# Scores of a gated linear recurrence: levels up to 8 from products of 32 tokens with 32, put together in a tile of 32 columns a chunk

## The chip, the cores and the metric

The kernel runs on one core of a Trainium2 chip. TensorE (PE) multiplies matrices, VectorE (DVE) and ScalarE (ACT) do elementwise work and read the products out of PSUM, GpSimd (POOL) does small side work, and SyncE (SP) issues the DMAs. The metric is the device time of one execution in microseconds (us), as the median of several runs.

## The reference

One decoder layer over 512 tokens with 16 meta tokens ahead of them, width 1024, float32. Two branches (a gated recurrence of 8 heads, and causal pooling) are merged by gates, and a SwiGLU feed-forward layer follows. The change lies in the recurrence, which for each head of 128 key and 128 value channels is:

```
S_t = diag(f_t) S_{t-1} + k_t v_t^T ;   o_t = S_t^T q_t
# in a chunk, for s <= t:
scores[t, s] = sum over channels d of  q[t, d] * k[s, d] * f[s+1, d] * ... * f[t, d]
o = scores @ v  +  (q * decay) @ S
```

The decay differs from channel to channel, so the scores of a chunk are no single matrix product.

## The kernel before, in words

**Scores by levels.** `hgrn(g)` treats a group of two heads; four groups follow each other. Tokens are cut into 4 chunks of 128 for each head, so a group has 8 tiles of 128 x 128 scores (index i), kept transposed as `scT`. They are built in levels h = 1, 2, 4, ..., 64. At level h a block of 2h tokens is split in two: the scores between its earlier half (keys) and its later half (queries) are one product of `kk` (keys with the decay up to the middle) and `Q` (queries with the decay from the middle). After each level `widen` multiplies the next decay into `kk` and `Q` in place (DVE, L465 and L467), so the product of the next level waits for it.

**Products.** At levels 16, 32 and 64 (L526) each block is a product of its own: h keys with h queries, `ps[b:b+h, ...]`, placed at the PSUM partitions where the block belongs. Blocks at other partitions then use other columns of the array. At levels 2, 4 and 8 the product is taken over the whole tile: all 128 keys of a chunk are the stationary operand (L513, L519) with 64 or 128 query columns, and most of what comes out lies outside the blocks. DVE then keeps the wanted entries with masks: `scT` is written by multiplies with `mask` (L548, L556) and by predicated copies (L559, L565). Level 1 holds the scores of a token with itself. These are sums over channels of `E` = q times k, taken by a product with `ones`; there `E` is split into a high part `Eh` and a rest `El` (ACT L486, DVE L487) and multiplied twice (L508, L509). `M2` holds the query columns of level 2. The masks are made once, at the start, by POOL (L90, L92).

**What sets the order.** A scheduler orders the instructions of each engine when the program is built. The source gives it the frame: `weave` puts one step of `hgrn` (one level) between every 6 to 9 steps of the large projections `product` (names `pj_...`, lines L156 to L158), each with weights read from DRAM (`wr`) and split into a high part by ACT (`wh`, L132) and a rest by DVE (`wl`, L139). The first projection and `make_masks` stand in a section in which the order is that of the source. PSUM tiles of the recurrence rotate over three banks (`psh`).

Of the kernel before, what the change touches and what calls it, by code (L numbers as in the profile page):

```python
# [8 lines left out]
F32 = mybir.dt.float32  # L9
F32R = mybir.dt.float32r  # L10
I32 = mybir.dt.int32
AF = mybir.ActivationFunctionType
ALU = mybir.AluOpType
AX = mybir.AxisListType

P = 128
D = 1024
T = 512
# [13 lines left out]
def f32(ap):  # L32
    return ap.bitcast(F32)
# [3 lines left out]
def hybrid_layer(ctx: ExitStack, tc: tile.TileContext, x, meta_tokens, norm_mix_g, w_in, lb_raw,  # L37
                 hgrn_norm_g, pool_w, pool_scale, w_branch_a, w_branch_b, w_out, norm_ffn_g,
                 w_ffn_gate, w_ffn_up, w_ffn_down, norm_final_g, out):
    nc = tc.nc  # L40
    cst = ctx.enter_context(tc.tile_pool(name="cst", bufs=1))
# [3 lines left out]
    sm = ctx.enter_context(tc.tile_pool(name="sm", bufs=2))  # L45
    psm = ctx.enter_context(tc.tile_pool(name="psm", bufs=5, space=bass.MemoryType.PSUM))
    psh = ctx.enter_context(tc.tile_pool(name="psh", bufs=3, space=bass.MemoryType.PSUM))
# [5 lines left out]
    def g4t(name, dt=F32, shape=(P, 1024)):  # L53
        return g4.tile(list(shape), dt, tag="g4", name=name)

    def t5(name, cols=T):
        return sm.tile([P, TT], F32, tag="t5", name=name, bufs=8)[:, 0:cols]

    def bank(pool, name):
        return pool.tile([P, 512], F32, tag=pool.name, name=name)  # L60
# [18 lines left out]

    mask = cst.tile([P, 5, 64], F32, name="mask")
    ones = cst.tile([P, P], F32R, name="ones")
    nc.vector.memset(f32(ones), 1.0)
    maski = mask.bitcast(I32)

    def keep(m, nb, h, step, lo, hi):

        m = m.rearrange("p (b h) -> p b h", h=h)
        nc.gpsimd.affine_select(out=m, in_=m, compare_op=ALU.is_ge, fill=0.0, base=-lo,  # L90
                                pattern=[[-step, nb], [0, h]], channel_multiplier=1)
        nc.gpsimd.affine_select(out=m, in_=m, compare_op=ALU.is_ge, fill=0.0, base=hi,  # L92
                                pattern=[[step, nb], [0, h]], channel_multiplier=-1)

    def make_masks():
        nc.gpsimd.memset(mask, 1.0)
        keep(mask[:, 0, :], 64, 1, 2, 0, 0)
        keep(mask[:, 1, :], 64, 1, 2, 0, 1)
        for li, h in enumerate((2, 4, 8)):
            keep(mask[:, 2 + li, :], 64 // h, h, 2 * h, 0, h - 1)  # L100


    class Weights:
# [266 lines left out]
    def first_product(done):  # L370
# [73 lines left out]
        for j in range(2):  # L444
            done(j, pss[j])
        make_masks()
        mk.__exit__(None, None, None)
        yield

    def halves(ap, h):  # L450
        v = ap.rearrange("p (b two h) -> p b two h", two=2, h=h)
        return v[:, :, 0, :], v[:, :, 1, :]

    def totals(t, h, n, out):

        a, b = halves(t, 1)
        nc.vector.tensor_mul(out, a[:, :, 0], b[:, :, 0])
# [11 lines left out]
    def hgrn(g):  # L469

        F, kk, qq, Fm, km, vt, vm = grp[g]
        scT, Q, tt = g4t(f"scT{g}"), g4t(f"Q{g}"), g4t(f"tt{g}")
# [3 lines left out]
            tot[h] = tt[:, off:off + 1024 // h]  # L476
            off += 1024 // h
        nc.vector.tensor_mul(Q, qq, F)
        M2 = g4t(f"M2{g}").rearrange("p (i c) -> p i c", c=P)
        E, Ehl = t5(f"E{g}"), g4t(f"Ehl{g}", F32R)  # L480
        Eh, El = Ehl[:, 0:T], Ehl[:, T:2 * T]
        qe, qo = halves(qq, 1)
        ke = halves(kk, 1)[0]
        per = lambda ap: ap.rearrange("p (i b) h -> p i b h", i=8)
        nc.vector.tensor_mul(E, qe[:, :, 0], ke[:, :, 0])
        nc.scalar.copy(out=Eh, in_=E)  # L486
        nc.vector.tensor_sub(El, E, f32(Eh))  # L487
        nc.scalar.copy(out=M2[:, :, 0:64], in_=per(qo)[:, :, :, 0])
        totals(F, 1, 1024, tot[2])
        kmf = km.rearrange("p a m -> p (a m)")  # L490
        tm = Fm.rearrange("p a m -> p (a m)")
# [10 lines left out]


        sc4 = scT.rearrange("p (i c) -> p i c", c=P)
        for h in (1, 2, 4, 8, 16, 32, 64):
            if h == 1:
                ps = bank(psh, f"psd{g}")
                nc.tensor.matmul(ps, ones, Eh, start=True, stop=False)  # L508
                nc.tensor.matmul(ps, ones, El, start=False, stop=True)  # L509
            elif h == 2:  # L510
                pss = [bank(psh, f"psc{g}_{h}{i}") for i in range(2)]
                for i in range(8):
                    nc.tensor.matmul(pss[i // 4][:, (i % 4) * P:(i % 4 + 1) * P], kk[:, i * P:(i + 1) * P],  # L513
                                     M2[:, i, :], start=True, stop=True)
            elif h <= 8:
                ps = bank(psh, f"psc{g}_{h}")
                q1 = halves(Q, h)[1].rearrange("p (i b) h -> p i b h", i=8)
                for i in range(8):
                    nc.tensor.matmul(ps[:, i * 64:(i + 1) * 64], kk[:, i * P:(i + 1) * P], q1[:, i],  # L519
                                     start=True, stop=True)  # L520
            else:
                ps = bank(psh, f"psc{g}_{h}")
                for i in range(8):
                    for b in range(0, P, 2 * h):
                        o = i * P + b
                        nc.tensor.matmul(ps[b:b + h, i * h:(i + 1) * h], kk[:, o:o + h],  # L526
                                         Q[:, o + h:o + 2 * h], start=True, stop=True)
            if h == 4:

                pk = bank(psh, f"pkm{g}")  # L530
                for hh in range(2):
                    nc.tensor.transpose(pk[:NM, hh * P:(hh + 1) * P], km[:, hh, :], ident)
                kmT = sm.tile([NM, 2 * P], F32, tag="kmT", name=f"kmT{g}", bufs=1)
                nc.vector.tensor_copy(kmT, pk[:NM, 0:2 * P])
            if h == 16:
                pS = bank(psh, f"pS{g}")
                for hh in range(2):
                    hs = slice(hh * P, (hh + 1) * P)
                    nc.tensor.matmul(pS[:, hs], kmT[:, hs], vm[:, hs], start=True, stop=True)
                S = sm.tile([P, 2 * P], F32, tag="S", name=f"S{g}_0", bufs=5)  # L540
                nc.vector.tensor_copy(S, pS[:, 0:2 * P])
                Ss = [S]
            widen(tot[h], h, kk, Q)
            if h > 1:
                totals(tot[h], h, 1024 // h, tot[2 * h])
            if h == 1:
                nc.scalar.copy(out=M2[:, :, 64:P].rearrange("p i (b h) -> p i b h", h=2), in_=per(halves(Q, 2)[1]))
                nc.vector.tensor_tensor(  # L548
                    sc4.rearrange("p i (b two) -> p i b two", two=2)[:, :, :, 0],
                    ps.rearrange("p (i b) -> p i b", i=8),  # L550
                    mask[:, 0, :].unsqueeze(1).to_broadcast([P, 8, 64]), ALU.mult)
            elif h == 2:
                for i in range(2):
                    o = sc4[:, 4 * i:4 * i + 4, :]
                    v = pss[i].rearrange("p (i two b) -> p i two b", i=4, two=2)
                    nc.vector.tensor_tensor(  # L556
                        o.rearrange("p i (b two) -> p i b two", two=2)[:, :, :, 1], v[:, :, 0, :],
                        mask[:, 1, :].unsqueeze(1).to_broadcast([P, 4, 64]), ALU.mult)
                    nc.vector.copy_predicated(  # L559
                        o.rearrange("p i (b two h) -> p i b two h", two=2, h=2)[:, :, :, 1, :],  # L560
                        maski[:, 2, :].rearrange("p (b h) -> p b h", h=2).unsqueeze(1).to_broadcast([P, 4, 32, 2]),
                        v[:, :, 1, :].rearrange("p i (b h) -> p i b h", h=2))
            elif h <= 8:
                li = {4: 3, 8: 4}[h]
                nc.vector.copy_predicated(  # L565
                    sc4.rearrange("p i (b two h) -> p i b two h", two=2, h=h)[:, :, :, 1, :],
                    maski[:, li, :].rearrange("p (b h) -> p b h", h=h).unsqueeze(1).to_broadcast([P, 8, 64 // h, h]),
                    ps.rearrange("p (i b h) -> p i b h", i=8, h=h))
            else:
                for b in range(0, P, 2 * h):  # L570
                    nc.scalar.copy(out=sc4[b:b + h, :, b + h:b + 2 * h],
                                   in_=ps[b:b + h, 0:8 * h].rearrange("p (i c) -> p i c", i=8))
            yield
# [17 lines left out]
        for c in range(3):  # L591
            S2 = sm.tile([P, 2 * P], F32, tag="S", name=f"S{g}_{c + 1}", bufs=5)
            for hh in range(2):
# [3 lines left out]
                    out=S2[:, hs], in0=Ss[c][:, hs], scalar=tot[128][:, e:e + 1],  # L597
# [7 lines left out]
        for cp in range(2):  # L605
            po = bank(psh, f"po{g}_{cp}")
            for c2 in range(2):
                c = 2 * cp + c2
                for hh in range(2):
# [4 lines left out]
                                     start=False, stop=True)  # L614
# [202 lines left out]
    for j in range(NF // 2):  # L817
# [7 lines left out]
        if j == 0:  # L825
            ws = [W.get(1 - i) for i in range(2)]
            pss = [bank(psm, f"pj_fg0{i}") for i in range(2)]
            for a in (0, 256):
                if a:
                    to_feature_major(n2[3], P, n2h, n2l, 3 * P, "h3")  # L830
                for i in range(2):
                    for k in range(KT):
                        w, cs = ws[k // 4], slice(i * P, (i + 1) * P)
                        mv, lv = N2(k)
# [84 lines left out]
```

## Time and profile before

| | |
|---|---|
| median of 3 runs | 874.63 us (872.34 to 874.73) |
| the profiled execution: its time, its span | 872.36 us, 870.6 us |
| PE busy with matmuls | 858.5 us (99% of the span), 4961 instructions |
| DVE, ACT, POOL busy | 391.7, 275.5, 28.8 us |
| DMA queue of the loads | 80.57 MB, 29.6% of 16 engines' span |

A busy share counts an engine as busy while it holds any instruction, so a PE at 99% is never without one, which is not the same as a PE at its peak: matmuls overlap in the array, and what one of them costs is how much later the next can start. One fp32 product of the source appears as two MATMUL records in the trace, each with a LDWEIGHTS of its own (PEld).

### The profile page before, as it was taken

The numbers are of one execution on the slowest core, as the hardware profiler recorded it, in microseconds if no ns is written. First come the engines' busy times: TensorE is split into PE (matmuls) and PEld (weight loads), VectorE is DVE, ScalarE is ACT, GpSimd is POOL, SyncE is SP. The second block draws the span as 40 slices with busy tenths as digits, with TensorE's granted clock in tenths as the row PEclk, the third lists the DMA queues.
The fourth block names the chain that finished last, engine by engine and source line by source line (L and its number), as shares of the span: only waits on it lengthen the run. The fifth ranks groups of instructions, "written<-read, shape, count | busy, mean of one in ns | idle before, by whom it ended". The sixth has DMA issues, their size and how long they took to land.

```text
span 870.6 us, 11703 instructions
## 1 busy us (share of the span) xinstructions
PE 858.5 (99%) x4961; PEld 732.2 (84%) x4961; DVE 391.7 (45%) x573; ACT 275.5 (32%) x416; POOL 28.8 (3%) x61
## 2 busy tenths in 40 slices
PE   7999999999999999999999999999999999999996
PEld 7999988898898888888888888888888888888885
DVE  5567537444753765544333643333333333323224
ACT  5433333233233234333331442222222222213111
POOL 4100010001001001000000100000000000000001
PEclk9999999999999999999999999999999999999999
DMA  7332122222222212233253143333333332323212
GB/s 257 97 97 70 54 73 73 73 78 69 74 74 72 74 49 77 94 97 97 96 216 99 51 120 97 96 97 96 90 89 91 96 96 97 122 97 96 97 49 97
DMA packets 68590, 81.31 MB, mean 93 GB/s; under 512 B 2573, under 2 KB 58410, under 8 KB 68538
## 3 DMA queue, kind: packets, MB, share of 16 engines
q1 hardware_dynamic: 68538, 80.57, 29.6%
q8 instruction: 39, 0.64, 0.3%
q14 instruction: 13, 0.11, 0.0%
HBM read 78.46 MB, written 2.10 MB: 93 GB/s over the span
## 4 chain that ended last, share of the span: by engine, by line
PE 95%; DVE 2%; ACT 1%; DMA 1%; issue 1%; POOL 1%; SPq 0%; POOLq 0%; DVEq 0%; ACTq 0%
PE pj_fu L157 5%; PE pj_fu L158 5%; PE pj_fu L156 5%; PE pj_fg L158 5%; PE pj_fg L156 5%; PE pj_fg L157 5%; PE pd L772 4%; PE pd L773 4%; PE pd L771 4%; PE pj_v L156 2%; PE pj_v L158 2%; PE pj_v L157 2%; PE pj_ga L157 2%; PE pj_gb L156 2%; PE pj_q L158 2%; PE pj_q L156 2%
## 5 line engine op out<-in xcount | busy, mean ns | idle before, releaser
L139 DVE TENSOR_TENSOR wl<-wr,wh 128x1024 fp32r<-128x1024 f32 x137 | 167.8, 1225 | 334.5 <-ACT wh L132 329.6
L132 ACT CAST wh<-wr 128x1024 fp32r<-128x1024 f32 x138 | 145.0, 1051 | 340.0 <-issue 93.3
L158 PE MATMUL pj_fg<-n2h,wl 128*128 128x512 f32 (+1 forms) x192 | 72.0, 375 | 0.2
L157 PE MATMUL pj_fg<-n2l,wh 128*128 128x512 f32 (+1 forms) x192 | 72.2, 376 | 0.0
L156 PE MATMUL pj_fg<-n2h,wh 128*128 128x512 f32 (+1 forms) x192 | 71.8, 375 | 0.2 <-ACT n2h L229 0.2
L157 PE MATMUL pj_fu<-n2l,wh 128*128 128x512 f32 x176 | 69.6, 395 | 0.0
L158 PE MATMUL pj_fu<-n2h,wl 128*128 128x512 f32 x176 | 69.2, 393 | 0.0
L156 PE MATMUL pj_fu<-n2h,wh 128*128 128x512 f32 x176 | 68.9, 393 | 0.0
L772 PE MATMUL pd<-wl,hidh 128*128 128x512 f32 (+1 forms) x176 | 66.2, 376 | 0.0
L771 PE MATMUL pd<-wh,hidh 128*128 128x512 f32 (+1 forms) x176 | 66.2, 376 | 0.0
L773 PE MATMUL pd<-wh,hidl 128*128 128x512 f32 (+1 forms) x176 | 66.1, 376 | 0.0
L156 PEld LDWEIGHTS pj_fg<-n2h,wh 128*128 128x128 f32 x192 | 36.0, 188 | 7.7 <-ACT n2h L229 0.5
L158 PEld LDWEIGHTS pj_fg<-n2h,wl 128*128 128x128 f32 x192 | 36.1, 188 | 7.4 <-DVE wl L139 0.6
L157 PEld LDWEIGHTS pj_fg<-n2l,wh 128*128 128x128 f32 x192 | 36.0, 188 | 7.2 <-DVE n2l L232 0.2
L156 PEld LDWEIGHTS pj_fu<-n2h,wh 128*128 128x128 f32 x176 | 33.0, 188 | 7.8
L157 PEld LDWEIGHTS pj_fu<-n2l,wh 128*128 128x128 f32 x176 | 33.0, 188 | 7.6
L158 PEld LDWEIGHTS pj_fu<-n2h,wl 128*128 128x128 f32 x176 | 33.1, 188 | 7.5
L771 PEld LDWEIGHTS pd<-wh,hidh 128*128 128x128 f32 x176 | 33.1, 188 | 6.2
L772 PEld LDWEIGHTS pd<-wl,hidh 128*128 128x128 f32 x176 | 33.1, 188 | 6.1
L773 PEld LDWEIGHTS pd<-wh,hidl 128*128 128x128 f32 x176 | 33.1, 188 | 6.0
L156 PE MATMUL pj_v<-nTh,wh 128*128 128x256 f32 (+1 forms) x128 | 36.9, 288 | 0.0
L158 PE MATMUL pj_v<-nTh,wl 128*128 128x256 f32 (+1 forms) x128 | 36.4, 284 | 0.0
(237 smaller groups left out, 1730.9 us busy)
## 6 DMA issues: line engine op xcount, KB each, us to landing
wr<-in_w_in_dram SPq DMA_DIRECT2D x52, 512.0 KB, 3.5
wr<-in_w_ffn_gate_dram SPq DMA_DIRECT2D x22, 512.0 KB, 3.7
wr<-in_w_ffn_up_dram SPq DMA_DIRECT2D x22, 512.0 KB, 3.8
wr<-in_w_ffn_down_dram SPq DMA_DIRECT2D x22, 512.0 KB, 3.4
wr<-in_w_branch_a_dram SPq DMA_DIRECT2D x8, 512.0 KB, 3.4
wr<-in_w_out_dram SPq DMA_DIRECT2D x8, 512.0 KB, 3.2
x<-in_x_dram SPq DMA_DIRECT2D x4, 512.0 KB, 5.5
wr<-in_w_branch_b_dram SPq DMA_DIRECT2D x4, 512.0 KB, 3.5
```

The lines of the kernel that those rows point to most:

```text
L132: nc.scalar.copy(out=h, in_=self.raw[i])
L139: eng.tensor_sub(l, self.raw[i], f32(self.parts[i][0]))
L156: nc.tensor.matmul(ps, sh, mh, start=first, stop=False)
L157: nc.tensor.matmul(ps, sh, ml, start=False, stop=False)
L158: nc.tensor.matmul(ps, sl, mh, start=False, stop=last)
L771: nc.tensor.matmul(pt, sh[:, cs], w[0][:, k, a:e], start=first, stop=False)
L772: nc.tensor.matmul(pt, sh[:, cs], w[1][:, k, a:e], start=False, stop=False)
L773: nc.tensor.matmul(pt, sl[:, cs], w[0][:, k, a:e], start=False, stop=last)
```

## The change

At levels 2, 4 and 8 each of the 32 windows of 32 tokens (8 tiles, 4 windows `c` each) gets a product of its own: 32 keys with 32 (level 2) or 16 query columns, written to the PSUM partitions 32c to 32c+31. So a level has 32 products in place of 8. Level 1 becomes four fp32 products of a 128 x 32 block of ones with a quarter of `E` each, and the split into `Eh` and `El` goes away. The results of levels 1 to 8 are put together in a new small tile `dS`, 128 partitions by 8 x 32 columns, with masks of 16 columns; after level 8 ACT copies it in four pieces onto the diagonal of `scT`, which POOL has set to zero before. The masks are made differently: POOL makes a 4 x 16 pattern `wide` for each mask in a tile with a single buffer, and DVE sums it to 16 columns.

```
     def make_masks():
-        nc.gpsimd.memset(mask, 1.0)
-        keep(mask[:, 0, :], 64, 1, 2, 0, 0)
...
+        for m, (h, step, hi) in enumerate(((1, 2, 0), (1, 2, 1), (2, 4, 1), (4, 8, 3), (8, 16, 7))):
+            wide = sm.tile([P, 4, 16], F32, tag="mw", name=f"mw{m}", bufs=1)
+            nc.gpsimd.memset(wide, 1.0)
...
+            nc.vector.reduce_sum(mask[:, m, :], wide.rearrange("p c b -> p b c"), axis=AX.X)
...
-        E, Ehl = t5(f"E{g}"), g4t(f"Ehl{g}", F32R)
-        Eh, El = Ehl[:, 0:T], Ehl[:, T:2 * T]
+        dS = t5(f"dS{g}", 256).rearrange("p (i c) -> p i c", c=32)
+        E = t5(f"E{g}")
...
-        nc.scalar.copy(out=Eh, in_=E)
-        nc.vector.tensor_sub(El, E, f32(Eh))
...
+        nc.gpsimd.memset(scT, 0.0)
+        wins = [(i, c) for i in range(8) for c in range(4)]
...
             if h == 1:
-                ps = bank(psh, f"psd{g}")
-                nc.tensor.matmul(ps, ones, Eh, start=True, stop=False)
-                nc.tensor.matmul(ps, ones, El, start=False, stop=True)
...
+                for c in range(4):
+                    nc.tensor.matmul(ps[32 * c:32 * c + 32, 0:P], ones, E.rearrange(
+                        "p (i w b) -> p i w b", i=8, w=4)[:, :, c, :], start=True, stop=True)
             elif h <= 8:
-                ps = bank(psh, f"psc{g}_{h}")
-                q1 = halves(Q, h)[1].rearrange("p (i b) h -> p i b h", i=8)
-                for i in range(8):
-                    nc.tensor.matmul(ps[:, i * 64:(i + 1) * 64], kk[:, i * P:(i + 1) * P], q1[:, i],
+                n = 32 if h == 2 else 16
+                for i, c in wins:
+                    o = (4 * i + c) * 32
+                    mv = M2[:, 4 * i + c, :] if h == 2 else halves(Q[:, o:o + 32], h)[1]
+                    nc.tensor.matmul(ps[32 * c:32 * c + 32, i * n:(i + 1) * n], kk[:, o:o + 32], mv,
                                      start=True, stop=True)
...
                 nc.vector.copy_predicated(
-                    sc4.rearrange("p i (b two h) -> p i b two h", two=2, h=h)[:, :, :, 1, :],
...
+                    dS.rearrange("p i (b two h) -> p i b two h", two=2, h=h)[:, :, :, 1, :],
+                    masked({2: 2, 4: 3, 8: 4}[h], h), v.rearrange("p i (b h) -> p i b h", h=h))
+                if h == 8:
+                    for c in range(4):
+                        nc.scalar.copy(out=sc4[32 * c:32 * c + 32, :, 32 * c:32 * c + 32],
+                                       in_=dS[32 * c:32 * c + 32])
```

PE's order in group 0 around level 2, first of before, then of the change (a name's trailing number counts tiles; `pj_p` are projections, a row without x is one product):

```order
L156 MATMUL pj_p_651<-nTh,wh_652 128x272
L157 MATMUL pj_p_651<-nTl,wh_652 128x272
L158 MATMUL pj_p_651<-nTh,wl_654 128x272
L513 MATMUL psc_20_763<-M_630,k_119 128x128 x4
L513 MATMUL psc_21_764<-M_630,k_119 128x128 x4
L156 MATMUL pj_p_650<-nTh,wh_652 128x256
```

```order
L154 MATMUL pj_p_663<-nTh,wh_664 128x272
L155 MATMUL pj_p_663<-nTl,wh_664 128x272
L156 MATMUL pj_p_663<-nTh,wl_666 128x272
L517 MATMUL psc_2_778<-M_644,k_119 32x32 x32
L154 MATMUL pj_p_662<-nTh,wh_664 128x256
L155 MATMUL pj_p_662<-nTl,wh_664 128x256
L156 MATMUL pj_p_662<-nTh,wl_666 128x256
```

Eight products with 128 result partitions have become 32 with 32, and they still stand in one piece between two projections.

PE's order in group 3 around level 1, before and after (`pj_gb` are projections of 512 columns):

```order
L158 MATMUL pj_gb_2944<-nTh,wl_2874 128x512
L508 MATMUL psd_2969<-Ehl_2927,ones 128x512
L156 MATMUL pj_gb_2943<-nTh,wh_2945 128x512
L157 MATMUL pj_gb_2943<-nTl,wh_2945 128x512
L158 MATMUL pj_gb_2943<-nTh,wl_2947 128x512
L156 MATMUL pj_gb_2943<-nTh,wh_2945 128x512
L509 MATMUL psd_2969<-Ehl_2927,ones 128x512
```

```order
L155 MATMUL pj_gb_3178<-nTl,wh_3108 128x512
L156 MATMUL pj_gb_3178<-nTh,wl_3110 128x512
L510 MATMUL psc_1_3204<-E_3163,ones 32x128 x4
L154 MATMUL pj_gb_3178<-nTh,wh_3108 128x512
L155 MATMUL pj_gb_3178<-nTl,wh_3108 128x512
```

The two products of level 1 with projections between them have become four in a row; counted from the last block of `pj_q`, they stand three projections earlier (after 21 in place of 24; in group 0 after 42 in place of 44).

DVE's order after the first projection, where the masks are made, first of before and then of the change (`km`, `tm` are small tiles of the meta tokens, `wl` the rest parts of weights):

```order
L331 TENSOR_SCALAR km_122<-Fm_121 128x16
L457 TENSOR_TENSOR tm_1_639<-Fm_121 128x16
L467 TENSOR_TENSOR km_122<-km_122,Fm_121 128x16
L457 TENSOR_TENSOR tm_2_642<-tm_1_639 128x8
L467 TENSOR_TENSOR km_122<-km_122,tm_1_639 128x8x2
L467 TENSOR_TENSOR km_122<-km_122,tm_2_642 128x4x4
L457 TENSOR_TENSOR tm_4_645<-tm_2_642 128x4
L467 TENSOR_TENSOR km_122<-km_122,tm_4_645 128x2x8
L139 TENSOR_TENSOR wl_546<-wr_432,wh_544 128x1024
```

```order
L98 TENSOR_REDUCE mask<-mw_412 128x16
L465 TENSOR_TENSOR km_122<-km_122,Fm_121 128x16
L455 TENSOR_TENSOR tm_1_651<-Fm_121 128x16
L465 TENSOR_TENSOR km_122<-km_122,tm_1_651 128x8x2
L455 TENSOR_TENSOR tm_2_654<-tm_1_651 128x8
L465 TENSOR_TENSOR km_122<-km_122,tm_2_654 128x4x4
L98 TENSOR_REDUCE mask<-mw_417 128x16
L455 TENSOR_TENSOR tm_4_657<-tm_2_654 128x4
L465 TENSOR_TENSOR km_122<-km_122,tm_4_657 128x2x8
L98 TENSOR_REDUCE mask<-mw_422 128x16
L98 TENSOR_REDUCE mask<-mw_427 128x16
L137 TENSOR_TENSOR wl_560<-wr_446,wh_558 128x1024
```

Five sums now stand among the small operations, four of them ahead of the weight part that stood behind those operations before and one behind it; each waits for POOL.

## Rows read from the trace of the kernel before

**Rows 1.** Page: the span, and its first part, busy us of each engine.
```profile
span 870.6 us, 11703 instructions
PE 858.5 (99%) x4961; PEld 732.2 (84%) x4961; DVE 391.7 (45%) x573; ACT 275.5 (32%) x416; POOL 28.8 (3%) x61
```

**Rows 2.** Waits of PE over the whole span: us in total, times, longest.
```profile
PE tp_x L224 <- DVE n_x L213: 2.1, 1, 2.1
```

**Rows 3.** Windows over the levels of the four groups; columns in the first row.
```profile
core 0: us, PE busy (x) PEld busy (x) DVE busy (x) ACT busy (x) POOL busy (x), PEclk, DMA share, GB/s
57.40:103.10 45.70, 45.70 (x456) 43.74 (x455) 36.07 (x68) 15.57 (x36) 0.00 (x0) 1.00 0.20 60
sum 176.60, PE 176.60 PEld 158.50 DVE 118.69 ACT 54.85 POOL 0.00; mean PE 44.15 PEld 39.62 DVE 29.67 ACT 13.71 POOL 0.00
```

**Rows 4.** Timeline of PE, level 2 of group 0.
```profile
63.15 0.29 PE L158 MATMUL pj_p<-nTh,wl 128*128 128x272 f32 x1
63.27 1.95 PE L513 MATMUL psc<-M,k 128*128 128x128 f32 x16
...
65.17 0.28 PE L157 MATMUL pj_p<-nTl,wh 128*128 128x256 f32 x1
65.29 0.28 PE L158 MATMUL pj_p<-nTh,wl 128*128 128x256 f32 x1
```

**Rows 5.** Timeline of PE around levels 4 (with pkm) and 8 of group 0.
```profile
70.05 0.28 PE L158 MATMUL pj_p<-nTh,wl 128*128 128x272 f32 x1
...
72.24 0.28 PE L157 MATMUL pj_p<-nTl,wh 128*128 128x256 f32 x1
...
77.08 0.29 PE L158 MATMUL pj_p<-nTh,wl 128*128 128x272 f32 x1
...
79.12 0.28 PE L157 MATMUL pj_p<-nTl,wh 128*128 128x256 f32 x1
```

**Rows 6.** Timeline of PE, level 1 of group 3.
```profile
289.55 0.40 PE L158 MATMUL pj_gb<-nTh,wl 128*128 128x512 f32 x1
289.79 0.39 PE L508 MATMUL psd<-Ehl,ones 128*128 128x512 f32 x1
290.02 0.40 PE L156 MATMUL pj_gb<-nTh,wh 128*128 128x512 f32 x1
```

**Rows 7.** Timeline of PE, level 32 of group 0 (two column positions).
```profile
90.79 0.29 PE L158 MATMUL pj_f<-nTh,wl 128*128 128x272 f32 x1
91.01 0.70 PE L526 MATMUL psc<-Q,k 128*32 128x32 f32 x32
91.64 0.39 PE L156 MATMUL pj_f<-nTh,wh 128*128 128x256 f32 x1
91.86 0.28 PE L157 MATMUL pj_f<-nTl,wh 128*128 128x256 f32 x1
```

**Rows 8.** Window over level 16 of group 0, L526 alone.
```profile
84.45:85.07 0.62, 0.62 (x64) 1.00 0.00 0
```

**Rows 9.** Timeline of PE, the first 0.21 us of that level.
```profile
84.45 0.37 PE L526 MATMUL psc<-Q,k 128*16 128x16 f32 x30
```

**Rows 10.** Timelines of DVE and PE: E of group 3, two weight parts, users.
```profile
288.27 0.69 DVE L485 TENSOR_TENSOR E<-q,k 128x512 f32<-128x512 f32 x1
...
35.41 1.23 DVE L139 TENSOR_TENSOR wl<-wr,wh 128x1024 fp32r<-128x1024 f32 x1 [1.63 <-ACT wh L132]
...
46.77 0.39 PE L156 MATMUL pj_q<-nTh,wh 128*128 128x512 f32 x1
...
83.06 1.22 DVE L139 TENSOR_TENSOR wl<-wr,wh 128x1024 fp32r<-128x1024 f32 x1
...
98.83 0.28 PE L156 MATMUL pj_v<-nTh,wh 128*128 128x256 f32 x1
```

**Rows 11.** Groups by form: a copy of ACT, mask work of POOL.
```profile
L571 ACT COPY scT<-psc 32x256 f32<-32x256 f32 x8 | 2.9, 364 | 3.0 <-PE psc L526 2.9
...
L90 POOL TENSOR_SCALAR_AFFINE_SELECT mask<-mask 128x64 f32<-128x64 f32 x5 | 2.8, 562 | 0.1
L96 POOL MEMSET mask<- 128x320 f32 x1 | 0.4, 357 | 0.0
```

More of the change, by code (lines that the diff above doesn't have):

```diff
@@ L78, in hybrid_layer @@
     nc.gpsimd.memset(mhalf, -0.5)
-    mask = cst.tile([P, 5, 64], F32, name="mask")
-    ones = cst.tile([P, P], F32R, name="ones")
-    nc.vector.memset(f32(ones), 1.0)
+    mask = cst.tile([P, 5, 16], F32, name="mask")
+    ones = cst.tile([P, 32], F32, name="ones")
+    nc.vector.memset(ones, 1.0)
     maski = mask.bitcast(I32)
[L87 to L93, printed above, removed]
-    def make_masks():
-        nc.gpsimd.memset(mask, 1.0)
-        keep(mask[:, 0, :], 64, 1, 2, 0, 0)
-        keep(mask[:, 1, :], 64, 1, 2, 0, 1)
-        for li, h in enumerate((2, 4, 8)):
-            keep(mask[:, 2 + li, :], 64 // h, h, 2 * h, 0, h - 1)
+    def make_masks():
+        for m, (h, step, hi) in enumerate(((1, 2, 0), (1, 2, 1), (2, 4, 1), (4, 8, 3), (8, 16, 7))):
+            wide = sm.tile([P, 4, 16], F32, tag="mw", name=f"mw{m}", bufs=1)
+            nc.gpsimd.memset(wide, 1.0)
+            v = wide.rearrange("p c (b h) -> p c b h", h=h)
+            for op_lo in (True, False):
+                nc.gpsimd.affine_select(out=v, in_=v, compare_op=ALU.is_ge, fill=0.0, base=0 if op_lo else hi,
+                                        pattern=[[-32, 4], [-step, 16 // h], [0, h]] if op_lo else
+                                        [[32, 4], [step, 16 // h], [0, h]],
+                                        channel_multiplier=1 if op_lo else -1)
+            nc.vector.reduce_sum(mask[:, m, :], wide.rearrange("p c b -> p b c"), axis=AX.X)
     class Weights:
@@ L478, in hgrn @@
         nc.vector.tensor_mul(Q, qq, F)
-        M2 = g4t(f"M2{g}").rearrange("p (i c) -> p i c", c=P)
-        E, Ehl = t5(f"E{g}"), g4t(f"Ehl{g}", F32R)
-        Eh, El = Ehl[:, 0:T], Ehl[:, T:2 * T]
+        M2 = g4t(f"M2{g}").rearrange("p (w c) -> p w c", c=32)
+        dS = t5(f"dS{g}", 256).rearrange("p (i c) -> p i c", c=32)
+        E = t5(f"E{g}")
         qe, qo = halves(qq, 1)
         ke = halves(kk, 1)[0]
-        per = lambda ap: ap.rearrange("p (i b) h -> p i b h", i=8)
         nc.vector.tensor_mul(E, qe[:, :, 0], ke[:, :, 0])
-        nc.scalar.copy(out=Eh, in_=E)
-        nc.vector.tensor_sub(El, E, f32(Eh))
-        nc.scalar.copy(out=M2[:, :, 0:64], in_=per(qo)[:, :, :, 0])
+        nc.scalar.copy(out=M2[:, :, 0:16], in_=qo[:, :, 0].rearrange("p (w b) -> p w b", b=16))
         totals(F, 1, 1024, tot[2])
@@ L504, in hgrn, with masked @@
         sc4 = scT.rearrange("p (i c) -> p i c", c=P)
+        nc.gpsimd.memset(scT, 0.0)
+        wins = [(i, c) for i in range(8) for c in range(4)]
+        def masked(m, h):
+            return maski[:, m, :].rearrange("p (b h) -> p b h", h=h).unsqueeze(1).to_broadcast([P, 8, 16 // h, h])
         for h in (1, 2, 4, 8, 16, 32, 64):
+            ps = bank(psh, f"psc{g}_{h}")
             if h == 1:
-                ps = bank(psh, f"psd{g}")
-                nc.tensor.matmul(ps, ones, Eh, start=True, stop=False)
-                nc.tensor.matmul(ps, ones, El, start=False, stop=True)
-            elif h == 2:
-                pss = [bank(psh, f"psc{g}_{h}{i}") for i in range(2)]
-                for i in range(8):
-                    nc.tensor.matmul(pss[i // 4][:, (i % 4) * P:(i % 4 + 1) * P], kk[:, i * P:(i + 1) * P],
-                                     M2[:, i, :], start=True, stop=True)
-            elif h <= 8:
-                ps = bank(psh, f"psc{g}_{h}")
-                q1 = halves(Q, h)[1].rearrange("p (i b) h -> p i b h", i=8)
-                for i in range(8):
-                    nc.tensor.matmul(ps[:, i * 64:(i + 1) * 64], kk[:, i * P:(i + 1) * P], q1[:, i],
+                for c in range(4):
+                    nc.tensor.matmul(ps[32 * c:32 * c + 32, 0:P], ones, E.rearrange(
+                        "p (i w b) -> p i w b", i=8, w=4)[:, :, c, :], start=True, stop=True)
+            elif h <= 8:
+                n = 32 if h == 2 else 16
[3 more added lines that the diff above has]
+                    nc.tensor.matmul(ps[32 * c:32 * c + 32, i * n:(i + 1) * n], kk[:, o:o + 32], mv,
                                      start=True, stop=True)
             else:
-                ps = bank(psh, f"psc{g}_{h}")
                 for i in range(8):
@@ L546, in hgrn @@
             if h == 1:
[L547 to L562, printed above, removed]
-            elif h <= 8:
-                li = {4: 3, 8: 4}[h]
-                nc.vector.copy_predicated(
-                    sc4.rearrange("p i (b two h) -> p i b two h", two=2, h=h)[:, :, :, 1, :],
-                    maski[:, li, :].rearrange("p (b h) -> p b h", h=h).unsqueeze(1).to_broadcast([P, 8, 64 // h, h]),
-                    ps.rearrange("p (i b h) -> p i b h", i=8, h=h))
@@ new lines, in hgrn @@
+                nc.scalar.copy(out=M2[:, :, 16:32].rearrange("p w (b h) -> p w b h", h=2),
+                               in_=halves(Q, 2)[1].rearrange("p (w b) h -> p w b h", b=8))
+                nc.vector.tensor_tensor(dS[:, :, 0:32:2], ps[:, 0:P].rearrange("p (i b) -> p i b", i=8),
+                                        mask[:, 0, :].unsqueeze(1).to_broadcast([P, 8, 16]), ALU.mult)
+            elif h <= 8:
+                v = ps[:, 0:256 if h == 2 else P].rearrange("p (i c) -> p i c", i=8)
+                if h == 2:
+                    nc.vector.tensor_tensor(dS[:, :, 1:32:2], v[:, :, 0:16],
+                                            mask[:, 1, :].unsqueeze(1).to_broadcast([P, 8, 16]), ALU.mult)
+                    v = v[:, :, 16:32]
+                nc.vector.copy_predicated(
+                    dS.rearrange("p i (b two h) -> p i b two h", two=2, h=h)[:, :, :, 1, :],
[4 more added lines that the diff above has]
+                                       in_=dS[32 * c:32 * c + 32])
```

## The prediction, made before the changed kernel ran

> **What bounds the kernel now.** I read the page first. PE is busy for 858.5 of 870.6 us [rows 1]; that alone does not bound a kernel, so I went to PE's waits. There are six rows, 5.0 us in all, the largest 2.1 us in the first microseconds [rows 2], and none of them is a wait of the recurrence's products. So PE's instruction stream is the end of every stage, and a microsecond taken out of it comes off the time, as long as no other engine falls behind. Next I looked at the stretches that the change touches, the levels of the four groups: PE is busy through all 176.60 us of them at a granted clock of 1.00 (the 2.4 GHz level), DVE for 118.69, ACT for 54.85, POOL for nothing [rows 3]. The reader should see that the other engines have room there, and that PE has none. Last I read single levels on PE's timeline. A busy time is of little use for them, since the records overlap. I take as the price of a level how much later the projections go on: from the start of the last projection ahead of it to the start of the second one behind it, less two ordinary steps of 0.12 us, which a projection of 256 columns takes (65.17 to 65.29 in [rows 4]; with 272 columns slightly more, so I take off 0.25 for both).
>
> **Prices before.** Level 2: 65.17 - 63.15 - 0.25 = 1.77 us for 16 records, 0.106 us each from 63.27 to the next projection [rows 4]. Level 4 with the two transposes of `pkm`: 72.24 - 70.05 - 0.25 = 1.94; level 8: 79.12 - 77.08 - 0.25 = 1.79 [rows 5]; so `pkm` is 0.15. Half as many columns in levels 4 and 8 buy nothing against level 2, which shows that the 128 stationary columns set the price there. Level 1 in group 3: 290.02 - 289.55 less one step of 0.23 is 0.24 us a product [rows 6], 0.48 for two. The other groups repeat these prices.
>
> **What a level of 32-token products costs.** The new levels have a near relative. Level 32 has 16 products, 32 records, with 32 stationary and 32 moving columns at two column positions of the array: 91.86 - 90.79 - 0.25 = 0.82 us, of which 0.63 lies between its first record and the next projection and 0.19 is going in and out [rows 7]. Level 16 has 64 records at four positions (16 stationary, 16 moving columns) and takes the same 0.62 us [rows 8]. Twice the records in the same time means that products at different positions run side by side: both levels have 16 records a position. The new levels 2, 4 and 8 have 64 records at four positions, again 16 a position; level 2 has level 32's shape, levels 4 and 8 lie between the two. I take 0.82 us for each. Lower bound: level 16's 0.62 + 0.19 = 0.81. Upper bound: the records keep level 32's mean pace however many positions there are, 0.63 / 32 = 0.02 us, 64 of them 1.26, with 0.19 added 1.45.
>
> **Level 1.** Four products, 8 records of 32 stationary and 128 moving columns. Side by side, two a position at level 2's 0.106: 0.21 + 0.19 = 0.40; one after another: 8 x 0.106 + 0.19 = 1.04. Since four positions overlap in [rows 8], I stay near the low end, 0.50, and count level 1 as unchanged against 0.48.
>
> **The sum.** Per group: level 2 gives 1.77 - 0.82 = 0.95, level 4 1.94 - 0.82 - 0.15 = 0.97, level 8 1.79 - 0.82 = 0.97, together 2.89; four groups 11.6 us. The profiled execution took 872.36 us and stands 2.3 below the median of the three runs, 874.63, beside the fastest of them, 872.34. So 860.8 on its own footing, 863.0 on the median's; I predict 862. With the lower bounds (0.81 three times, level 1 at 0.40) a group gains 3.0 and the time is 860.3 on the profile's footing; with both upper bounds it gains 0.32 + 0.34 + 0.34 less 0.56 for level 1, 0.44, and the time is 870.6, or 872.9 on the median's.
>
> **What lies beside it.** DVE loses the `El` subtraction and most of the elements of the mask steps, and gains only five small sums at the start; it is hidden by PE anyway. POOL's zeroing of `scT` has 1024 columns; `mask` with 320 took 0.36 us [rows 11], so about 1.2 us by proportion, on an engine that has nothing to do in these stretches and whose result is first wanted at level 8. ACT loses a cast and gains four copies a group of 32 x 256, 0.36 each [rows 11], 1.5 us. Behind them in ACT's queue stands a weight's high part, and behind that DVE's rest. In group 0 the rest part in that place was written from 83.06 to 84.28 and first used at 98.83 [rows 10]; 14.5 us cover it. Were that cover gone, the 1.5 us would fall on PE, 6 us over four groups.
>
> **The places where a wait could come up.** First the masks. `wide` has one buffer, so POOL may begin the next mask only when DVE has summed the last, and DVE's small operations and a weight part (wl, 35.41) queue behind sums that wait for POOL. A round is two selects of 0.56 us [rows 11], and a memset no dearer than `mask`'s 0.36: up to 1.5 us. Three rounds stand ahead of the weight part, less what the small operations between them use. It will be up to 4 us late, ending at 40.6 instead of 36.6; its block begins on PE at 46.77 [rows 10]. Hidden, with 6 us to spare. Second, `E` in group 3: DVE ends it at 288.27 + 0.69 = 288.96 [rows 10], and PE, three projections of 0.23 earlier than the 289.79 of [rows 6], wants it at 289.10. This is tight: 0.1 to 0.3 us could be lost there once. What the faster levels make late next is the `widen` of DVE, which starts earlier with them, and it stays behind PE by the same projections as before.
>
> **A rule against the change.** The row first: 30 records of level 16 start within its first 0.21 us [rows 9], 7 ns apart. The Trainium skill ("TensorE: Matmul & The Clock Gate", section "Back-to-back issue gap") gives starts of small matmuls a floor of about 25 ns, however few the columns. By it 64 records would take 1.6 us, a level 1.79, and nothing would be gained: about 872 on the profile's footing. The trace disagrees with it at several column positions, which is why the sum goes by the rows.
>
> **Rivals.** (a) Overlap in part. After its first 30 records level 16 slows: the other 34 share 0.62 - 0.21 = 0.41 us, 12 ns each, so the quick start may be only what stood ready ahead of time. With 32 stationary columns the second half could fall to level 32's 20 ns: 0.21 + 34 x 0.02 + 0.19 = 1.08 a level, 0.26 worse three times, 3.1 us in four groups: 864 to 866; at the upper bounds 870.6 to 872.9. Against it: at four positions 20 ns is 80 ns for a position, and level 32 does one in 40. (b) New waits eat the gain, by the E and ACT places above: 0.3 + 6 us, 867 to 869. Against it: the covers. (c) Slower: the positions do not overlap with 32 stationary columns. Then 64 records at level 32's pace for one position, 0.63 / 16 = 0.04 us, take 2.52 + 0.19 = 2.71, 0.93 more than before; twelve levels 11.2, and level 1 at 1.04 adds 2.2: 886. It decides from 25 ns a record, (1.79 - 0.19) / 64, where gain turns to loss. Against it: level 16's 64 records in 0.62 us, 10 ns each, and level 32's 20. (d) No change: the pace lies just at that 25 ns, about 872 to 875. This is the case that the floor of the Trainium skill would give. Against it: the same rows.
>
> **How the numbers follow.** My forecast, a gain of 10 to 13 us, 0.70 (860 to 864 by footing); (a) 0.17; (b) 0.05; (c) 0.04; (d) 0.04. The predicted time is the forecast's, 862. The range 859.5 to 868 holds the forecast, the nearer part of (a) and half of (b), about 0.82. What a measurement here can tell from no change is about 0.3%, 2.6 us; (a) at its far end falls within it, a small part. Faster 0.92, same 0.04, slower 0.04.
>
> **What would show it.** Right: the records of the new lines hold 32 columns, each of levels 2, 4 and 8 keeps PE from projections for 0.8 to 0.9 us, level 1 for about 0.5 at one place; PE's waits show no new row above 0.5 us; the span falls by about 11.6 us, all of it between 57 and 310 us. Wrong by (a): these levels cost 1.0 to 1.45. By (b): PE waits for E, a weight part or `dS`. By (c): levels of 2.7 us. Anything that moves the time behind the recurrence would be outside this account.

## The result, and the profile after

The changed kernel takes 863.09 us (861.95 to 863.82, 4 runs), the kernel before beside it 874.68 (872.34 to 874.94, 4 runs). The ratio is 0.987, 95% interval 0.985 to 0.989. The profiled execution took 862.53 us with a span of 860.8, which is 9.8 less than in [rows 1].

The page of the change begins with the span and the busy times of the engines:

```profile
span 860.8 us, 12910 instructions
PE 848.8 (99%) x5561; PEld 717.9 (83%) x5561; DVE 380.6 (44%) x566; ACT 280.1 (33%) x428; POOL 33.8 (4%) x69
```

PE has 600 records more than in [rows 1] and is busy for 9.7 us less. PE's waits, in us, times and longest, are again six rows with 5.1 us in all:

```profile
PE tp_x L222 <- DVE n_x L211: 2.4, 2, 2.0
PE warm L376 <- POOL ident masks.py:199: 1.4, 1, 1.4
PE tp_x L222 <- DVE nTl L230: 0.5, 1, 0.5
PE tp_x L222 <- DVE mt L428: 0.4, 1, 0.4
PE pj_fg L154 <- ACT n2h L227: 0.2, 1, 0.2
PE pj_fg L156 <- DVE wl L137: 0.2, 1, 0.2
```

None of them is a wait of a level, of `E`, or of `dS`. The timeline of PE shows the levels of group 0 (1, 2, 4 with `pkm`, 8), which answer to [rows 4, 5], each between the projection ahead and the second one behind; the last three rows are level 1 of group 3, which answers to [rows 6]:

```profile
58.26 0.29 PE L156 MATMUL pj_p<-nTh,wl 128*128 128x272 f32 x1
58.48 0.43 PE L510 MATMUL psc<-E,ones 128*32 128x128 f32 x8
...
59.06 0.28 PE L155 MATMUL pj_p<-nTl,wh 128*128 128x256 f32 x1
...
63.91 0.29 PE L156 MATMUL pj_p<-nTh,wl 128*128 128x272 f32 x1
64.13 0.76 PE L517 MATMUL psc<-M,k 128*32 128x32 f32 x64
...
65.05 0.28 PE L155 MATMUL pj_p<-nTl,wh 128*128 128x256 f32 x1
...
69.90 0.29 PE L156 MATMUL pj_p<-nTh,wl 128*128 128x272 f32 x1
70.11 0.74 PE L517 MATMUL psc<-Q,k 128*32 128x16 f32 x64
70.78 0.38 PE L529 MATMUL pkm<-ident,km 128*16 128x128 f32 x2
...
71.12 0.28 PE L155 MATMUL pj_p<-nTl,wh 128*128 128x256 f32 x1
...
75.97 0.29 PE L156 MATMUL pj_p<-nTh,wl 128*128 128x272 f32 x1
76.19 0.74 PE L517 MATMUL psc<-Q,k 128*32 128x16 f32 x64
...
77.08 0.28 PE L155 MATMUL pj_p<-nTl,wh 128*128 128x256 f32 x1
...
281.65 0.40 PE L156 MATMUL pj_gb<-nTh,wl 128*128 128x512 f32 x1
281.98 0.43 PE L510 MATMUL psc<-E,ones 128*32 128x128 f32 x8
...
282.67 0.40 PE L155 MATMUL pj_gb<-nTl,wh 128*128 128x512 f32 x1
```

Read as in the prediction (start of the second projection behind, less the start of the one ahead, less two ordinary steps), level 2 costs 65.05 - 63.91 - 0.25 = 0.89 us, level 4 with `pkm` 71.12 - 69.90 - 0.25 = 0.97, level 8 77.08 - 75.97 - 0.25 = 0.86, and level 1 0.55 in group 0 (59.06 - 58.26 - 0.25) and 0.56 in group 3 (282.67 - 281.65 - 0.46). The other groups repeat these within 0.03. The same reading of all four groups in both traces (less 0.46 where projections of 512 columns stand on both sides, 0.35 at the one level that has them on one side) gives:

| level | before, four groups | after | gained |
|---|---|---|---|
| 1 | 2.15 us | 2.21 | -0.1 |
| 2 | 7.14 | 3.57 | 3.6 |
| 4 with pkm | 7.79 | 3.93 | 3.9 |
| 8 | 7.14 | 3.44 | 3.7 |
| sum | 24.22 | 13.15 | 11.1 |

So the levels gave back 11.1 us, yet the span fell by 9.8. Laid beside each other, the two projection streams show where the rest is: at the first `tp_m`, 20 us after the start, the changed kernel is 0.9 us behind (20.86 against 19.96 us); at its last level it is 9.9 ahead, and it stays so to the end. The loss thus lies in the first 20 us, which the prediction had not looked at. In these two executions it goes with PE's clock. The windows from 12 to 17 us (columns as in [rows 3]), first of before, then of the change:

```profile
12.00:17.00 5.00, 5.00 (x40) 4.79 (x41) 3.64 (x6) 4.39 (x8) 2.84 (x5) 1.00 1.05 325
```

```profile
12.00:17.00 5.00, 5.00 (x29) 4.77 (x29) 3.64 (x7) 4.45 (x7) 2.83 (x5) 0.66 0.94 312
```

PE ran at the 2.4 GHz level through all of it in the one profile, and for two thirds of it at the 1.2 GHz level in the other (0.66), with 40 records against 29 in the same 5 us. Ahead of the fall PE had stood still for 2.0 us, waiting for `n_x`; but it did so in both. By 17 us the changed kernel was 1.4 us behind: a block of the first projection that starts at 15.67 us in before starts at 17.05. Before then lost 0.4 of that again, since its `tp_m` waited for `n_m`, and the late one did not. First before, then the change:

```profile
19.96 0.63 PE L429 MATMUL tp_m<-ident,n_m 16*128 16x16 f32 x8 [0.37 <-DVE n_m L420]
```

```profile
20.86 0.66 PE L427 MATMUL tp_m<-ident,n_m 16*128 16x16 f32 x8
```

A second difference cost nothing in this execution, because PE was late, but it costs time in others (below). It is a pair of instructions on DVE and POOL. First DVE's `n_m`, for which PE's `tp_m` waits, and POOL's first select in the trace of before:

```profile
19.08 0.74 DVE L420 TENSOR_SCALAR n_m<-xm,r_m 16x1024 f32<-16x1024 f32 x1
...
18.86 0.36 POOL L96 MEMSET mask<- 128x320 f32 x1
19.29 1.05 POOL L90 TENSOR_SCALAR_AFFINE_SELECT mask<-mask 128x64 f32<-128x64 f32 x1
```

And in that of the change:

```profile
18.94 1.22 DVE L418 TENSOR_SCALAR n_m<-xm,r_m 16x1024 f32<-16x1024 f32 x1
...
18.72 0.14 POOL L91 MEMSET mw<- 128x64 f32 x1
18.94 1.75 POOL L94 TENSOR_SCALAR_AFFINE_SELECT mw<-mw 128x64 f32<-128x64 f32 x2
```

The new memset has 64 columns in place of 320, so POOL comes to its first select 0.2 us earlier, in the same moment in which `n_m` begins, and `n_m` takes 1.22 us in place of 0.74. Where `n_m` was first, it was the select that took long (1.05).

### The profile page after: what moved, and what is told of

It reads as the page before. It is cut to its first block, busy times and chain, and to the rows that moved or that the text cites. A ratio compares the mean times of both kernels' runs of the same rounds, so it can differ in the third digit from the quotient of the medians.

```text
span 860.8 us, 12910 instructions
## 1 busy us (share of the span) xinstructions
PE 848.8 (99%) x5561; PEld 717.9 (83%) x5561; DVE 380.6 (44%) x566; ACT 280.1 (33%) x428; POOL 33.8 (4%) x69
## 4 chain that ended last, share of the span: by engine, by line
PE 96%; DVE 1%; DMA 1%; POOL 1%; ACT 0%; issue 0%; SPq 0%; POOLq 0%; ACTq 0%
PE pj_fu L155 5%; PE pj_fu L156 5%; PE pj_fu L154 5%; PE pj_fg L156 5%; PE pj_fg L155 5%; PE pj_fg L154 5%; PE pd L763 4%; PE pd L765 4%; PE pd L764 4%; PE pj_gb L154 2%; PE pj_v L154 2%; PE pj_v L156 2%; PE pj_v L155 2%; PE pj_gb L155 2%; PE pj_ga L155 2%; PE pj_q L156 2%
```

## The experiments

All are edits of the changed kernel, if nothing else is said. Times are medians, each beside runs of the kernel before on the same chip.

**Does the gain come from products at four positions side by side?** The same 32 products a level, in another order: all eight of one column position, then all of the next.

```diff
-        wins = [(i, c) for i in range(8) for c in range(4)]
+        wins = [(i, c) for c in range(4) for i in range(8)]
```

> Levels 2, 4 and 8 issue the same 32 products, but all 8 of one column position before the next position; nothing else differs. Theory (the gain is products running side by side at four positions): a position takes a record every 0.032 us, which the records of level 2 show (quartets of 32 ns at the start of the level in the changed kernel's trace), so 64 records one behind the other take 2.05 us and a level 2.3 to 2.4 us instead of 0.86 to 0.99; 1.45 more, twelve times 17 us: about 880, slower than before the change. Rival (the gain is smaller products, fewer columns, whatever runs beside what): 863, unchanged.

Measured: 876.77 us, ratio 1.004 (1.0025 to 1.0055). The gain is gone. PE's timeline, level 2 of group 0:

```profile
63.92 0.29 PE L156 MATMUL pj_p<-nTh,wl 128*128 128x272 f32 x1
64.14 1.91 PE L517 MATMUL psc<-M,k 128*32 128x32 f32 x64
65.98 0.39 PE L154 MATMUL pj_p<-nTh,wh 128*128 128x256 f32 x1
66.20 0.28 PE L155 MATMUL pj_p<-nTl,wh 128*128 128x256 f32 x1
```

The level costs 66.20 - 63.92 - 0.25 = 2.03 us with the same 64 records, 1.84 / 64 = 29 ns each. The sign is that of the theory; the level is cheaper than I had expected, so the time is 3 us lower. Within a position the records do start 32 ns apart; at the three changes of position the last of one and the first of the next overlap, which brings the mean down to 29.

**Two positions at a time:**

```diff
-        wins = [(i, c) for i in range(8) for c in range(4)]
+        wins = [(i, c) for p in (0, 2) for i in range(8) for c in (p, p + 1)]
```

> The same products in an order that alternates between two column positions, first 0 and 1, then 2 and 3. Theory (side by side, 32 ns a record and position): 16 ns a record, 64 records 1.02 us, a level 1.3 to 1.4 us; 0.45 more twelve times, 5.4 us: 868.5. Rival (smaller products alone): 863. Rival (positions do not matter, only that neighbours in the queue differ in position): 863.

Measured: 867.59 us, ratio 0.9936 (0.9919 to 0.9952). PE's timeline, the same level:

```profile
64.78 0.29 PE L156 MATMUL pj_p<-nTh,wl 128*128 128x272 f32 x1
65.00 1.11 PE L517 MATMUL psc<-M,k 128*32 128x32 f32 x64
66.04 0.39 PE L154 MATMUL pj_p<-nTh,wh 128*128 128x256 f32 x1
66.27 0.28 PE L155 MATMUL pj_p<-nTl,wh 128*128 128x256 f32 x1
```

1.24 us a level, 1.04 / 64 = 16 ns a record. One position at a time, two in turn and four in turn give 2.03, 1.24 and 0.89 us, with 16 records at each position in all three: the price goes by how many positions take turns.

**Is the pace lasting, or only a stock that stood ready?** Each level's products issued twice, all 32 and then all 32 again.

```diff
-                for i, c in wins:
+                for i, c in wins + wins:
```

> The 32 products of each of levels 2, 4 and 8 are issued twice, all 32 and then all 32 again with the same operands to the same place, so that the work is doubled and the result stays. Theory: what sets the pace is 8 to 8.35 ns a record with four positions side by side (32 ns a position, or the pairs of 16.7 ns in the second half of a level), without end; then 64 more records cost 0.51 to 0.53 us a level, levels of 1.38 to 1.43, and twelve of them 6.1 to 6.4 us: 869.3 to 869.5. The rival: the quick pace holds only for a stock of records that stands ready ahead of the level, and records behind it fall to the pace of one issue after the other, 16 to 25 ns; then 64 more cost 1.0 to 1.6 us a level and the time is 875 to 882.

Measured: 869.71 us, ratio 0.9958 (0.9945 to 0.9970); the change unaltered on that chip 862.28 (below). PE's timeline:

```profile
64.03 0.29 PE L156 MATMUL pj_p<-nTh,wl 128*128 128x272 f32 x1
64.25 1.30 PE L517 MATMUL psc<-M,k 128*32 128x32 f32 x128
...
65.70 0.29 PE L155 MATMUL pj_p<-nTl,wh 128*128 128x256 f32 x1
```

The level costs 65.70 - 64.03 - 0.25 = 1.42 us. The 64 further records cost 1.42 - 0.89 = 0.53 us, 8.3 ns each, and the theory held. Four positions at 8.3 ns, two at 16 and one at 32 are the same thing: a position takes a record of 32 stationary columns every 32 to 33 ns.

**Is it the products alone?** Levels 2, 4 and 8 get the products of before (128 keys of a chunk), and DVE takes the wanted 32 x 32 blocks out of them into `dS`; the rest stays as changed.

```diff
-                for i, c in wins:
-                    o = (4 * i + c) * 32
...
+                for i in range(8):
...
+                    nc.tensor.matmul(pss[i * n // 512][:, o:o + n], kk[:, i * P:(i + 1) * P], mv,
                                      start=True, stop=True)
```

> Only the products of levels 2, 4 and 8 go back to 8 over whole tiles of 128 keys; the assembly in the small tile, its masks, level 1 and the copies onto the diagonal stay as changed (DVE picks each quarter's columns with ops of 32 partitions, more and smaller ones). Theory: levels 2, 4 and 8 cost 1.78, 1.95 and 1.79 us again, 2.76 more a group, 11 us in all: 874, as before the change. Rival (the assembly or level 1 made the gain): 863 to 866.

Measured: 873.77 us, ratio 1.0003 (0.9994 to 1.0012), its levels at the prices of before (level 8 1.79). The new masks, `dS`, the copies and level 1 without its split give and cost nothing that this interval (0.8 us to either side) can tell; the products are the whole gain to within that. The run with a granted clock of 0.998 took 873.13 us, runs of before with the same 872.4 to 872.5; in its profile PE waits 0.84 us for `n_m`, in before 0.37.

**Is the work beside it hidden?** POOL's zeroing of `scT`, ACT's four copies and DVE's predicated copies are done three times.

```diff
-        nc.gpsimd.memset(scT, 0.0)
+        for _ in range(3):
+            nc.gpsimd.memset(scT, 0.0)
...
-                    for c in range(4):
+                    for c in [0, 1, 2, 3] * 3:
```

> The changed kernel with the side work of the score assembly tripled: the zeroing of scT on POOL, the four copies onto the diagonal on ACT, and each predicated copy on DVE are done three times with the same data. That is about 2.9 us more on ACT, 2 us on DVE and 1.9 us on POOL a group. Theory (PE alone ends every stage): 863, within 1.5 us, and PE's waits as before. Rival (part of the gain came from the lighter DVE, whose busy time fell by 11 us): some 8 us of it come back, 868 to 871, with waits of PE for DVE or ACT.

Measured: 864.35 us, ratio 0.9897 (0.9883 to 0.9912). Levels 1 to 8 keep their prices, and PE's waits have two new rows:

```profile
PE pj_f L154 <- ACT u L636: 1.2, 1, 1.2
PE tp_m L427 <- DVE n_m L418: 0.8, 1, 0.8
```

The first is ACT's queue: after level 8 of group 0, with eight further copies in it (twelve take 5.1 us, the four of the change 1.7), PE waited once for a copy out of PSUM, that of `u`. So the work of the change has cover, but not much more than its own size on ACT. The second row is the `n_m` of above, in a run in which PE was early enough to wait for it (0.4 us in before).

**Going in and out once less.** Level 1's four products directly ahead of those of level 2, in unused columns of the same bank.

```diff
...
+                    nc.tensor.matmul(ps[32 * c:32 * c + 32, 256:256 + P], ones, E.rearrange(
...
-                    nc.tensor.matmul(ps[32 * c:32 * c + 32, 0:P], ones, E.rearrange(
...
```

> The four products of level 1 move from their own place to directly ahead of those of level 2, into unused columns of the same PSUM bank; nothing is left out. If a stay in the small column positions has a fixed price for going in and out of about 0.3 us beside its records (level 2's 0.90 less 64 records at 8.35 ns leaves 0.36), the two levels cost 0.56 + 0.90 - 0.3 = about 1.15 us together and each group saves 0.3 us, 1.2 us in all: about 861.9 where the changed kernel has 863.1. The rival: the price of level 1 is that of its 8 records (0.07 us each), the two prices add up to 1.45 and the time stays at 863.

> The changed kernel unaltered, as the yardstick for the other two on this chip: 863.1 us, ratio to before 0.987; levels 2 to 8 at 0.86 to 0.90 us, with 0.12 more where pkm is.

Measured: 862.23 us (861.07 to 862.36) against 862.28 (862.00 to 863.75) for the change unaltered; ratios to before 0.9867 and 0.9870. In the trace the saving is there; PE's timeline of the two levels together:

```profile
64.66 0.29 PE L156 MATMUL pj_p<-nTh,wl 128*128 128x272 f32 x1
64.88 0.43 PE L510 MATMUL psc<-E,ones 128*32 128x128 f32 x8
65.12 0.74 PE L519 MATMUL psc<-M,k 128*32 128x32 f32 x64
...
66.02 0.28 PE L155 MATMUL pj_p<-nTl,wh 128*128 128x256 f32 x1
```

66.02 - 64.66 - 0.25 = 1.11 us where the two cost 0.55 + 0.89 = 1.44; 0.33 a group, 1.3 us in all. The medians don't show it. The profiled executions do: the granted clock from 12 to 18 us is 0.50 in this one and 0.51 in that of the change unaltered, and they took 862.33 and 863.75 us, 1.4 apart. But two of the four unaltered runs had a mean granted clock of 0.998 (862.00 and 862.01) and none of these had more than 0.996. The next experiments are therefore on the start.

**PE kept busy at the start.** Twelve idle transposes more, ten of them in the wait for `n_x`.

```diff
-        for i in range(30):
+        for i in range(32):
             nc.tensor.transpose(warm[:, 0:P], ident, ident)
...
+        for i in range(10):
+            nc.tensor.transpose(pss[0][0][:, 0:P], ident, ident)
```

> The changed kernel with twelve more idle transposes of the unit matrix at the start: two behind the 30 that are there, and ten into the 2.0 us in which PE waits for n_x; nothing else is altered. In the profile of the change PE runs at a granted clock of 0.66 (partly the 1.2 GHz level) from 12 to 17 us, in that of before at 1.00, and the start there cost 0.9 us. Theory: the runs of one kernel differ by up to 2.5 us because the wait there sometimes ends in the low level; with PE kept busy the granted clock is 1.00 over 12 to 17 us in every run, and the time is 861.6 us with a spread under 1 us. The rival: the level falls anyhow, or the fillers delay the first projection by as much; then 862.3 to 863.1 as before, with a spread of 2 us.

> The products of level 1 stand directly ahead of those of level 2, with the same twelve idle transposes at the start. In the trace of the kernel without the fillers the two levels cost 1.11 to 1.13 us together, where they cost 0.56 + 0.90 apart: 0.34 us a group, 1.35 in all, yet the medians on that chip were 862.23 and 862.28. Theory: the 1.35 us is real and the start hid it, so this kernel is 1.0 to 1.4 us below the change with fillers: 860.3 us. The rival: the 1.35 us is given back somewhere behind the levels, and the two are within 0.3 us of each other.

> The kernel before with the same twelve idle transposes at the start and nothing else altered. Theory: it comes to 872.3 us, the fastest of its runs, with a spread under 1 us, and the change with fillers is 10.8 us below it, which is what the four groups gain by their levels (11.1 by the trace). The rival: 873.4 and a spread of 2.5 us as without fillers.

Measured: the change with fillers 862.92 us (862.08 to 863.30), with level 1 at level 2 as well 861.84 (860.60 to 862.42), before with fillers 872.37 (872.25 to 874.08, 11 runs; without them 873.37 there, 15 runs, ratio 0.9994, 0.9985 to 1.0003). The first expectation fell: the change with fillers still shows a granted clock of 0.66 from 12 to 17 us in its profile, and its spread is 1.2 us. The second held in the distance, 1.1 us, but not in the time, 861.84 for 860.3. The third met its median, but not its spread (1.8 us) nor its distance to the change with fillers (9.5 us for 10.8). For before the fillers may help; the interval doesn't settle it. What does hold is a sorting of the runs by mean granted clock. Where it was 0.998 or 0.999 over the whole span, before takes 872.3 to 872.5 us, the change 862.0 to 862.1, the change with level 1 at level 2 860.6 (one run). At an equal start the change is thus worth about 10.3 us, and the joined levels 1.4.

**The select behind n_m.** POOL sets the first pattern three times in place of once, so that `n_m` begins first.

```diff
-            nc.gpsimd.memset(wide, 1.0)
+            for _ in range(3 if m == 0 else 1):
+                nc.gpsimd.memset(wide, 1.0)
```

> The changed kernel, in which POOL sets the first mask pattern to one three times in place of once, so that its first select begins about 0.3 us later; nothing else is altered. In the change DVE's n_m and POOL's first select begin in the same moment and n_m takes 1.22 us; in the kernel before n_m begins 0.2 us ahead of the select and takes 0.74, and PE's tp_m waits for n_m. Theory: whichever of the two begins first goes on alone and the other waits; then n_m takes 0.74 again, PE goes on 0.48 us earlier and the time is 0.5 us below the change: about 862.0 where the change has 862.3 to 863.1, 861.5 where PE's granted clock is 1.00 from the start. The rival: n_m is longer for another reason (its place, its input), takes 1.22 again, and nothing changes.

> The same two further settings of the first mask pattern, in the kernel in which level 1 stands directly ahead of level 2 (862.23 us by itself); nothing else is altered. If both terms are real they add up: 1.35 + 0.48 = 1.8 us below the change, about 861.0 as a median and 860.2 for a run with a granted clock of 1.00 from the start. The rival: the start's clock covers them and the median is 862 or more.

Measured: 863.12 us (862.58 to 863.97) in the changed kernel, and 861.04 (860.03 to 861.19), ratio 0.9858 (0.9843 to 0.9873), in the one with joined levels. DVE, POOL and PE in the profile of the second:

```profile
19.00 0.73 DVE L419 TENSOR_SCALAR n_m<-xm,r_m 16x1024 f32<-16x1024 f32 x1
...
18.79 1.05 POOL L92 MEMSET mw<- 128x64 f32 x3
19.91 1.43 POOL L95 TENSOR_SCALAR_AFFINE_SELECT mw<-mw 128x64 f32<-128x64 f32 x2
...
19.88 0.64 PE L428 MATMUL tp_m<-ident,n_m 16*128 16x16 f32 x8 [0.36 <-DVE n_m L419]
```

`n_m` takes 0.73 us again in both kernels, as the theory had it; now POOL was held up, whose third memset, beside `n_m`, took 0.64 us where the first took 0.14. In the first its time did not move: the profile shows PE at 0.66 from 12 to 17 us, `tp_m` only at 20.90 and no wait for `n_m`, so that PE's own lateness covered what was gained. In the second PE was on time (1.00), and its `tp_m` stands at 19.88, before's 19.96 and not the 20.41 of the same kernel with fillers and the early select. Its fastest run, 860.03, is 0.57 below that kernel's 860.60, one run each. It is the fastest kernel of the study.

## Why the prediction was right

Forecast 862.0, measured 863.09, by the mechanism that the forecast named; its steps one by one:

**PE's stream is the bound, and the levels are paid in it.** Right. The whole-tile kernel has all else of the change and none of the gain; the levels' 11.1 us less the 0.9 of the start is the span's fall to within 0.4 us.

**0.82 us a level.** Mis-sized a little: levels 2 and 8 cost 0.89 and 0.86; over the twelve levels it makes 0.5 us. The lower bound took level 16 as the relative, whose first 30 records start within 0.21 us [rows 9]. Level 2's timeline over the same 0.21 us holds fewer:

```profile
64.13 0.40 PE L517 MATMUL psc<-M,k 128*32 128x32 f32 x24
```

In that stretch every fourth record, the next one at the same position, starts 25 ns later with 16 stationary columns and 32 ns later with 32 (in level 8 as well, which has 16 moving columns like level 16). Level 32 had shown the 32, had I taken the starts at one position and not the mean with the time of leaving in it. Behind the first 32 records both levels go on at 9 to 10 ns.

**Level 1 unchanged at 0.50.** Nearly: 0.55 to 0.56 in place of 0.46 to 0.48 in three groups. In group 0 the two products of before stood apart and cost 0.74, so that the four groups together lose only 0.06.

**What lies beside it is hidden.** Right for `scT`, ACT's copies and DVE's masks (the kernel with three times of each). The masks' rounds did hold up DVE: its weight part was written from 38.90 to 40.11 us, 3.5 later than in [rows 10], and its block began on PE at 46.92, without a wait. `E` in group 3 was done at 281.07 + 0.68 = 281.75, PE came to it at 281.98: tight, and no wait. For ACT the step had named the wrong neighbour: not the weight part with its 14.5 us of cover gave way first, but the copy of `u` in the same queue, which had about 2.2 by an estimate (3.4 us of further copies made PE wait 1.2). What the step did not see is also the first select beside `n_m`: it counted POOL's work by POOL's time and asked who waits for its result, not which instruction of DVE it stands beside. That cost 0.48 us where PE was on time, and nothing where it was late.

**The span falls by 11.6.** 9.8; 11.1 from the levels, and the start took some back. Medians, which mix starts of both kinds, differ by 11.6 on the one chip and by 11.2 on the next (873.45 and 862.28); at equal starts it is about 10.3. That the first pair of medians differs by just the forecast's 11.6 is luck.

**The rivals.** (a) was true in shape: the second half of a level is slower than its first 32 records, but at 9 to 10 ns and not 20. (b) did not come. (c) is the right mechanism for products that follow each other at one position: the first experiment made it happen, at 2.03 us a level and not 2.71, since a position takes a record in 32 ns and not in 40. (d) did not come: the doubled level's 64 further records follow each other in 8.3 ns, not 25. The Trainium skill ("TensorE: Matmul & The Clock Gate", section "Back-to-back issue gap") has about 25 ns between starts as a floor. For products at several positions the 8.3 ns speak against it; at one position the 29 ns a record stay above it, and the trace doesn't contradict.

## What to carry to other kernels

Small fp32 products are cheap when neighbours in PE's order go to different column positions, and dear when they stay at one: where all four positions take turns, count the records of one position (33 ns each with 32 stationary columns); where one position follows the other, count them all. Add about 0.35 us for going in and out (an estimate: 0.89 - 64 x 0.0083 = 0.36, and joining two levels saved 0.33), and put neighbours of that kind together. When a side engine's work is moved or shortened, look also at which instruction of DVE it now begins beside. And where the runs of a kernel differ by 2 us, compare runs with an equal start before a median's tenth is believed.

## What was unexpected of the hardware

DVE and POOL held each other up: `n_m` 0.74 us when it began 0.2 us ahead of POOL's select, 1.22 when both began together, 0.73 when the select was put behind. The Trainium skill ("SBUF — State Buffer", section "Who interferes with whom") says that the two share a pair of ports, that whichever instruction takes it first keeps it to its end and the other stands, and that copies and `tensor_scalar` on DVE can be of the kind that takes it. These rows agree.

PE's level at the start is not settled. The wait of 2.0 us ahead of 12 us is the same in all kernels without the fillers, and some executions go on at 2.4 GHz (1.00 from 12 to 17 us in before) and others fall to 1.2 for a part of it (0.66 in the change) or for all of it (0.50 with the joined levels). Runs of one kernel lie up to 2.4 us apart (872.26 to 874.66 in before), the slower ones at the lower granted clocks. Filling that wait with transposes did not reliably prevent it, and no run here told what does.
